# Attention shares: two tiles for the transposed blocks, later products, and reciprocals in pairs

## The chip, the cores and the metric

The kernel runs on one core of one Trainium2 chip. The metric is device time in microseconds (us) of one launch, as the median of several runs. The engines are named as in the profile: PE multiplies matrices (PEld is its weight load), DVE is the vector engine, ACT the scalar engine, POOL the GpSimd engine, and SP the engine on whose queue most DMAs are issued.

## What is computed

One encoder layer over 512 tokens and 16 learned meta tokens (528 keys) of width 2048, all in float32. Two groups of eight heads share one input projection: mixer A (grouped-query attention with normalised, rotated queries and keys) and mixer B (differential attention with a distance penalty). Each head's output is gated, all are projected once, normalised and added to the input.

```python
hn = rmsnorm(h, pre_norm_g)                       # h: 16 meta tokens + 512 tokens, 2048 wide
qa, ka, va, ga, qb, kb, vb, gb = split(hn @ w_in)
# mixer A, 8 heads of 128, 2 heads of keys and values
q, k = rope(rmsnorm(qa, q_g)), rope(rmsnorm(ka, k_g))
oa = softmax(q @ k.T / sqrt(128)) @ va
# mixer B, 8 heads, two score maps each
bias = -slope * abs(qpos - kpos)
a = softmax(q1 @ k1.T / 8 + bias) - lam * softmax(q2 @ k2.T / 8 + bias)
ob = rmsnorm(a @ vb, sub_g) * (1 - lambda_init)
y = concat(oa * silu(ga), ob * silu(gb)) @ w_out
out = h + rmsnorm(y, post_norm_g)                 # of the 512 tokens
```

## The kernel before

**Products.** Every float32 operand is split into a high part, which ACT rounds (`hi`, L337), and a rest, which DVE subtracts (`lo`, L340). A product is then three matmuls: high by high, rest by high, high by rest. Weights arrive in chunks of 512 KB: SP loads a chunk into the tile `st` (L149), ACT writes its high part `wh` (L156), DVE its rest `wl` (L157). Each of the three names has three buffers, and a chunk is asked for two chunks ahead of its use. The list `splits` holds the two instructions of every weight split in the order in which they are recorded.

**Stages.** A first block of projections up to about 40 us; then the eight heads of mixer B, each beside the projections of the next head (`dense_T`, written as `pd`); then the eight heads of mixer A beside their query projections and gates; from about 786 us the output projection (`po`).

**One head.** The 512 queries are taken in four tiles of 128 (`t`), two tiles to a half. For each tile PE writes scores into the only score buffer `sc`; DVE adds the penalty, stores them as `p` and takes the row maximum (L519 in mixer B, L618 in mixer A), which frees `sc`; ACT takes the exponential and its sum (L527, L621). In mixer B there are two score groups to a tile, and the shares of the two maps are joined by POOL (L532) and DVE (L534). DVE then transposes `p` in 32 by 32 blocks into the tile `pt` (L448, and L450 for the 16 meta keys). When both tiles of a half stand in `pt`, `regroup` writes `pt` to the DRAM tile `turn` (L455), reads it back in four pieces as `pl` (L461), and its meta block as `pmf` (L462): so the blocks land with the keys on the partitions. `pt` and `pmf` have one buffer each, `pl` has two.

**Shares by values.** `p_times_v` splits `pl` into `ph` (ACT, L337) and `pl` (DVE, L340), and the meta block into `pm`; then it multiplies them with the values: 13 matmuls `pv`, broken up by other work. In mixer B a head ends with `finish_B`: the squares of its output are summed by two matmuls `ss`, ACT takes the root (L559), DVE four reciprocals of 128 columns each (L562) and two products (L563, L564), and SP stores the gated head `gB` (L566).

**What sets the order.** PE's order is written out by the class `Lanes`: all matmuls stay in program order, and a clock that only counts matmul time decides when the next step of a head (a generator) is recorded between the matmuls of the projections. The waits of these steps are the numbers of `LAG`: `pB` and `pA` between the end of a half and the start of `p_times_v`, `pvB` and `pvA` between its splits and its matmuls, `scB` between score groups. SP's weight loads stay in program order too (`load`). On ACT, DVE, POOL and for the other DMAs the order is a scheduler's, which goes by priorities; weight splits have a raised one (`rank`). `tc.issue_after(x)` places the instructions of its block behind `x` on the engine of `x`. Each engine works through its own list in order, so that an instruction that waits holds up all behind it.

Of the kernel before, what the change touches and what calls it, by code (L numbers as in the profile page):

```python
# [10 lines left out]
F32 = mybir.dt.float32  # L11
F32R = mybir.dt.float32r
F16 = mybir.dt.float16
AF = mybir.ActivationFunctionType
ALU = mybir.AluOpType
AX = mybir.AxisListType

P = 128
# [10 lines left out]
DW = NT + (TT - 1) * P  # L29


LAG = dict(vals=3.5, bank=2.8, bankA=1.5, bankB=2.5, turnA=1.5, turnB=1.5, pvA=5.5, pvB=6.0, scB=3.0,
           pB=14.0, ss=6.0, qA=2.35, scA=5.1, pA=11.5, rope=10.2, head=3.85, fin=1.35, qn=1.4, norm=4.0, valsA=(10.0, 7.0),
           steps=(3.0, 2.5, 2.0, 2.0), stepsK=(2.5, 2.0, 1.5))

AHEAD = -60
# [70 lines left out]
def kernel(ctx: ExitStack, tc: tile.TileContext, xT, xn, xm, w_s, w_t, w_q, w_o,  # L107
                             gpre, gq, gk, lams, gsub, gpost, ident_d, cos_d, sin_d, dist_d, out):
    nc = tc.nc
# [12 lines left out]
    ap = att.enter_context(tc.tile_pool(name="ap", bufs=2))  # L122
# [38 lines left out]
    splits = []  # L161
# [101 lines left out]
    for t in (TT, 0, 1, 2, 3):  # L263
        rows = P if t < TT else NM
        src = xn[t * P:(t + 1) * P, :] if t < TT else xm
        for j in range(2 if t < 2 else 4):

            tag, w = ("pl", "ph")[j % 2], 1024
            if t >= 2:
                tag, w = ("f", "g", "ql")[t - 2], 512  # L270
            st = (gp if tag == "g" else ap).tile([P, w], F32, name="xns", tag=tag,
                                                 bufs=2 if t < 2 else 4)[:rows]
            load(st, src[:, j * w:(j + 1) * w])
            acc = ssx[:, t, j:j + 1] if t < TT else ssm[:, j:j + 1]
            if j % 2:
                nc.vector.tensor_tensor_reduce(out=st, in0=st, in1=st, scale=1.0, scalar=0.0,
                                               op0=ALU.mult, op1=ALU.add, accum_out=acc)
            else:
                nc.scalar.activation(st, st, AF.Square, accum_out=acc)
# [9 lines left out]
                            op0=ALU.mult)  # L289
# [46 lines left out]
    def hi(dst, src):  # L336
        nc.scalar.activation(dst, src, AF.Copy)  # L337
# [89 lines left out]
        return g  # L427


    pv_last = [None]  # L430
    pv_open = [False]

    def whole():
# [18 lines left out]
    def regroup(pt):  # L452

        turn = dr.tile([P, 1088], F32, name="turn", tag="turn", bufs=3)
        nc.sync.dma_start(out=turn, in_=pt)  # L455
        turn = turn.rearrange("(i k) r -> k i r", i=4)
        pl = ap.tile([P, 1024], F32R, name="pl", tag="pl")
        pm = ap.tile([32, 2 * P], F32, name="pmf", tag="pmf", bufs=1)
        quad = pl.bitcast(F32).rearrange("p (i r) -> p i r", i=4)
        for m in range(4):  # L460
            nc.sync.dma_start(out=quad[32 * m:32 * m + 32], in_=turn[:, :, 256 * m:256 * m + 256])  # L461
        nc.sync.dma_start(out=pm.rearrange("p (i r) -> p i r", i=4), in_=turn[:, :, 1024:])  # L462
        return pl, pm

    def p_times_v(regrouped, v, done, gate_of):

        vh, vl, vm = v
        ab = "B" if gate_of is None else "A"
        pl, pf = regrouped
        ph = ap.tile([P, 1024], F32R, name="ph", tag="ph")  # L470
        pm = ap.tile([96, 2 * P], F32R, name="pm", tag="pm", bufs=1)
        pt = pl.bitcast(F32)
        hi(ph, pt)
        lo(pl, pt, ph)
        hi(pm[0:32], pf)
        nc.gpsimd.tensor_scalar(out=pm[32:64], in0=pm[0:32].bitcast(F32), scalar1=1.0,  # L476
                                scalar2=1.0, op0=ALU.mult, op1=ALU.mult)
        lo(pm[64:96], pf, pm[0:32])
        yield LAG["pv" + ab]
        while gate_of is not None and not place(gate_of):  # L480
            yield 0.3
        pv_open[0] = True
        pv = ptr.tile([P, 512], F32, name="pv", tag="tr")
        o = pv[:, :2 * P]
        ph, pl = [t.rearrange("p (i c r) -> p c i r", i=4, c=TT) for t in (ph, pl)]
        for c in range(TT):
            mm(o, vh[:, c, :], ph[:, c], start=(c == 0), stop=False)
            mm(o, vl[:, c, :], ph[:, c], start=False, stop=False)
            mm(o, vh[:, c, :], pl[:, c], start=False, stop=False)
            if c % 2:  # L490
                yield 0.0
        mm(o, vm, pm, start=False, stop=True)
        pv_open[0] = False
        done(o)
# [7 lines left out]
    def attention_B(h, qs, ks, v, v_task):  # L502
        o = ap.tile([P, SEQ], F32, name="oB", tag="f", bufs=4)
        last = None
        for half in range(2):
            pt = ap.tile([P, 1088], F32, name="pt", tag="pt", bufs=1)
            for t in (2 * half, 2 * half + 1):
                tq = slice(t * P, (t + 1) * P)
                mx = ap.tile([P, 2], F32, name="mx", tag="mx", bufs=4)
                sm = ap.tile([P, 2], F32, name="sm", tag="sm", bufs=4)  # L510
                p2 = []
                for m, ((q, ql), s) in enumerate(zip(qs, ks)):
                    sc = psc.tile([P, 2, 512], F32, name="sc", tag="sc")
                    for i, (n0, n1) in enumerate(KEYS):
                        mm(sc[:, i, :HALF], q[:, tq], s[:, n0:n1], start=True, stop=False)
                        mm(sc[:, i, :HALF], ql[:, tq], s[:, n0:n1], start=False, stop=True)
                    p = ap.tile([P, NT], F32, name="p", tag="p", bufs=4)
                    w0 = 3 * P - 32 * t
                    nc.vector.tensor_tensor_reduce(  # L519
                        out=two(p), in0=sc[:, :, :HALF], in1=two(dist[:, w0:w0 + NT]),  # L520
                        scale=-0.125 / slope(h), scalar=3.0e38, op0=ALU.add, op1=ALU.min,
                        accum_out=mx[:, m:m + 1])
                    p2.append(p)
                    if m == 0:
                        yield LAG["scB"]
                for m in range(2):
                    nc.scalar.activation(p2[m], p2[m], AF.Exp, scale=-1.0,  # L527
                                         bias=mx[:, m:m + 1], accum_out=sm[:, m:m + 1])
                nc.vector.reciprocal(out=sm, in_=sm)  # L529
                c2 = ap.tile([P, 1], F32, name="c2", tag="c2", bufs=4)  # L530
                nc.vector.tensor_tensor(out=c2, in0=sm[:, 1:2], in1=nlam, op=ALU.mult)
                nc.gpsimd.tensor_scalar(out=p2[0], in0=p2[0], scalar1=sm[:, 0:1], scalar2=1.0,  # L532
                                        op0=ALU.mult, op1=ALU.mult)
                nc.vector.scalar_tensor_tensor(out=p2[0], in0=p2[1], scalar=c2, in1=p2[0],  # L534
                                               op0=ALU.mult, op1=ALU.add)
                turned(pt, p2[0], t % 2)
                if t % 2 == 0:
                    yield LAG["scB"]
            last = spawn_pv(v_task, p_times_v(regroup(pt), v, lambda pv, half=half:
                            nc.scalar.activation(half_of(o, half), by_quad(pv), AF.Copy), None),  # L540
                            LAG["pB"])
            if half == 0:
                yield LAG["scB"]
        over[h] = lanes.spawn(finish_B(h, o), LAG["fin"], last)

    def finish_B(h, o):
# [12 lines left out]
        nc.scalar.activation(sq, ss, AF.Sqrt, scale=1.0 / P, bias=epst)  # L559
        for t in range(TT):  # L560
            tq = slice(t * P, (t + 1) * P)
            nc.vector.reciprocal(out=sq[:, tq], in_=sq[:, tq])  # L562
        nc.vector.tensor_tensor(out=o, in0=o, in1=sq, op=ALU.mult)  # L563
        nc.vector.scalar_tensor_tensor(out=gB[h], in0=o, scalar=sgc, in1=gB[h],  # L564
                                       op0=ALU.mult, op1=ALU.mult)
# [25 lines left out]
    def attention_A(h, qn, q_task, k, k_task, v, v_task):  # L591
# [12 lines left out]
        kh, kl = k  # L604
        last = None
        for half in range(2):
            pt = ap.tile([P, 1088], F32, name="pt", tag="pt", bufs=1)
            for t in (2 * half, 2 * half + 1):
                tq = slice(t * P, (t + 1) * P)
                mx = ap.tile([P, 1], F32, name="mxA", tag="mx", bufs=4)  # L610
# [2 lines left out]
                for i, (n0, n1) in enumerate(KEYS):  # L613
# [1 line left out]
                    mm(sc[:, i, :HALF], qh[:, tq], kl[:, n0:n1], start=False, stop=False)  # L615
                    mm(sc[:, i, :HALF], ql[:, tq], kh[:, n0:n1], start=False, stop=True)
                p = ap.tile([P, NT], F32, name="p", tag="p", bufs=4)
                nc.vector.tensor_tensor_reduce(  # L618
                    out=two(p), in0=sc[:, :, :HALF], in1=two(zed[0][:, :NT]), scale=-ASCALE,
                    scalar=3.0e38, op0=ALU.add, op1=ALU.min, accum_out=mx)  # L620
                nc.scalar.activation(p, p, AF.Exp, scale=-1.0, bias=mx, accum_out=sm)  # L621
                nc.vector.reciprocal(out=sm, in_=sm)
                nc.gpsimd.tensor_scalar(out=p, in0=p, scalar1=sm, scalar2=1.0,
# [18 lines left out]
    def squares(raw, n, rows=P):  # L642
        ss = ap.tile([P, 4], F32, name="ssh", tag="ssh", bufs=4)
        for i in range(n):
            jk = ap.tile([P, P], F16, name="jk", tag="jk", bufs=1)
            nc.scalar.activation(jk[:rows], raw[:, i, :], AF.Square, accum_out=ss[:rows, i:i + 1])
        rstd(ss[:rows, :n], ss[:rows, :n], P, rows)
        return ss
# [596 lines left out]
```

## Time and profile before

| | us |
|---|---|
| median of 3 runs (lowest to highest) | 953.71 (953.40 to 954.62) |
| the profiled execution: time | 949.57 |
| the profiled execution: span, first to last instruction | 947.8 |
| PE busy, weight loads busy | 888.2, 782.6 |
| DVE, ACT, POOL busy | 631.9, 497.1, 130.2 |
| mean granted clock of PE | 0.978 |

The page of the profile gives these sums, a strip of the span in 40 slices, and the chain of waits that ended last. Three further views of the trace are used: the waits by engine (who waited for whom, how long in total, how often, the longest one), the timeline of one engine (each instruction with its start, its duration, and in brackets the idle time before it and what ended it), and windows (busy time of each engine in a stretch, with the granted clock of PE; 0.50 is half speed). A matmul's shown duration is modelled; its cost in a stream is the distance to the next start. PE's line of 94% does not mean that 94% of the span is needed.

### The profile page before, as it was taken

The page shows a single profiled execution, that of the slowest core. Times are in us where ns is not written, and L with a number is a line of the kernel's source. Part 1 is how long each engine was busy: PE and PEld are TensorE (multiplying, and loading weights), DVE is VectorE, ACT ScalarE, POOL GpSimd, SP SyncE. Part 2 cuts the span into 40 slices and gives each one's busy share as a digit, 9 for nine tenths or more (in the row PEclk, how much of TensorE's full clock was granted, in tenths as well). Part 3 has the DMA queues.
Part 4 walks back from the last instruction along what each step waited for, and adds up shares of the span by engine and source line. Part 5 has one row for each costly group of instructions (what it writes and reads, how often), then busy time and mean ns, then how long its engine had stood idle before and what let it go on. Part 6 is the DMA issues. An engine that isn't in the chain of part 4 may idle for free.

```text
span 947.8 us, 14079 instructions
## 1 busy us (share of the span) xinstructions
PE 888.2 (94%) x5130; PEld 782.6 (83%) x5130; DVE 631.9 (67%) x1137; ACT 497.1 (52%) x845; POOL 130.2 (14%) x168
## 2 busy tenths in 40 slices
PE   9999888989989899898998999998999799999996
PEld 8898787888978889788888888997888587888885
DVE  6586674756657557575576546678766575886786
ACT  6464553635527346363464353555757455764561
POOL 0102110021110211102101020224122110000010
PEclk9999999899999999999999999999999899999999
DMA  9838648596784867848634333454657557989884
GB/s 338 271 114 247 182 136 225 144 252 181 206 228 132 246 176 192 249 140 218 188 101 141 98 89 99 160 176 138 161 161 224 156 171 273 328 284 311 272 263 155
DMA packets 80677, 185.49 MB, mean 196 GB/s; under 512 B 15136, under 2 KB 38560, under 8 KB 80224
## 3 DMA queue, kind: packets, MB, share of 16 engines
q1 hardware_dynamic: 75856, 167.81, 54.2%
q0 software_dynamic: 4608, 16.78, 10.4%
q8 instruction: 40, 0.66, 0.3%
q14 instruction: 29, 0.24, 0.1%
q10 hardware_dynamic: 144, 0.01, 0.0%
HBM read 158.34 MB, written 59.77 MB: 230 GB/s over the span
## 4 chain that ended last, share of the span: by engine, by line
PE 60%; DMA 14%; DVE 12%; ACT 6%; issue 4%; POOL 2%; SPq 2%; DVEq 0%; ACTq 0%; POOLq 0%
PE pd L61 36%; PE po L61 15%; DMA turn<-pt 7%; PE pv L61 4%; DMA pl<-turn 4%; PE sc L61 4%; DVE sq L562 2%; DVE wl L157 2%; ACT ph L337 1%; DMA st<-in_w_t_dram 1%; DVE pt L448 1%; SPq L461 1%; DVE pl L340 1%; DMA ws<-in_w_o_dram 1%; DMA ws<-ws 1%
## 5 line engine op out<-in xcount | busy, mean ns | idle before, releaser
L61 PE MATMUL pd<-xh,wh 128*128 128x264 f32 (+1 forms) x992 | 330.5, 333 | 6.4 <-ACT wh L156 6.4
L61 PE MATMUL pd<-xl,wh 128*128 128x264 f32 (+1 forms) x992 | 327.4, 330 | 0.4 <-DVE xl L192 0.4
L61 PE MATMUL pd<-xh,wl 128*128 128x264 f32 (+1 forms) x992 | 326.1, 329 | 0.0
L157 DVE TENSOR_TENSOR wl<-st,wh 128x1024 fp32r<-128x1024 f32 (+2 forms) x159 | 191.4, 1205 | 101.4 <-ACT wh L156 100.4
L156 ACT ACTIVATE wh<-st 128x1024 fp32r<-128x1024 f32 (+2 forms) x159 | 165.0, 1040 | 178.4 <-PE pd L61 83.8
L61 PEld LDWEIGHTS pd<-xh,wh 128*128 128x128 f32 x992 | 190.4, 192 | 19.7 <-ACT wh L156 6.8
L61 PEld LDWEIGHTS pd<-xh,wl 128*128 128x128 f32 x992 | 189.7, 191 | 17.1 <-DVE wl L157 0.9
L61 PEld LDWEIGHTS pd<-xl,wh 128*128 128x128 f32 x992 | 190.4, 192 | 12.0 <-DVE xl L192 0.6
L527 ACT ACTIVATE p<-p,mx 128x528 f32<-128x528 f32 x64 | 47.1, 736 | 75.3 <-DVE mx L519 74.5
L448 DVE STREAM_TRANSPOSE pt<-p 128x512 f32<-128x512 f32 x64 | 45.3, 707 | 30.3 <-DMA turn<-pt 18.9
L61 PE MATMUL pv<-ph,vh 128*128 128x256 f32 x128 | 38.5, 301 | 16.0 <-ACT ph L337 13.3
L519 DVE CUSTOM_DVE_ANT_0 p<-sc,dist 128x528 f32<-128x528 f32 x64 | 44.7, 698 | 11.7 <-PE sc L61 11.6
L340 DVE TENSOR_TENSOR pl<-pl,ph 128x1024 fp32r<-128x1024 f32 x32 | 39.5, 1233 | 17.4 <-ACT ph L337 17.2
L61 PE MATMUL pd<-wh,xh 128*128 128x512 f32 x128 | 50.5, 394 | 0.0
L337 ACT ACTIVATE ph<-pl 128x1024 fp32r<-128x1024 f32 x32 | 33.6, 1049 | 32.0 <-DMA pl<-turn 32.0
L61 PE MATMUL pd<-wl,xh 128*128 128x512 f32 x128 | 49.9, 390 | 0.0
L61 PE MATMUL pd<-wh,xl 128*128 128x512 f32 x128 | 49.9, 390 | 0.0
L532 POOL TENSOR_SCALAR p<-p,sm 128x528 f32<-128x528 f32 x32 | 24.1, 752 | 183.7 <-DVE sm L529 183.7
L61 PE MATMUL pv<-pl,vh 128*128 128x256 f32 x128 | 39.3, 307 | 10.6 <-DVE pl L340 10.6
L476 POOL TENSOR_SCALAR pm<-pm 32x256 fp32r<-32x256 f32 x32 | 29.0, 906 | 134.9 <-ACT pm L337 98.7
L621 ACT ACTIVATE p<-p,mxA 128x528 f32<-128x528 f32 x32 | 23.6, 736 | 43.8 <-DVE mxA L618 43.6
L61 PE MATMUL sc<-s,q 128*128 128x264 f32 x128 | 35.7, 299 | 11.4 <-DVE mx L519 8.6
(223 smaller groups left out, 1562.8 us busy)
## 6 DMA issues: line engine op xcount, KB each, us to landing
st<-in_w_t_dram SPq DMA_DIRECT2D x82, 512.0 KB, 5.4
turn<-pt SPq DMA_DIRECT2D x32, 544.0 KB, 3.1
ws<-in_w_o_dram POOLq DMA_DIRECT2D x32, 512.0 KB, 8.5
pl<-turn SPq DMA_DIRECT2D x128, 128.0 KB, 4.0
st<-ws SPq DMA_DIRECT2D x32, 512.0 KB, 4.5
st<-in_w_o_dram SPq DMA_DIRECT2D x22, 512.0 KB, 4.6
ws<-in_w_o_dram SPq DMA_DIRECT2D x16, 512.0 KB, 5.3
ws<-ws SPq DMA_DIRECT2D x16, 512.0 KB, 5.1
```

Of the source, the lines that this page charges most:

```text
L61: self._add(self.nc.tensor.matmul(out, lhsT, rhs, start=start, stop=stop, **kw), us)
L156: splits.append((nc.scalar.activation(wh[:, c], st[:, c], AF.Copy), nc.vector.tensor_tensor(out=wl[:, c], in0=st[:, c], in1=wh[:, c].bitca ...
L157: nc.vector.tensor_tensor(out=wl[:, c], in0=st[:, c], in1=wh[:, c].bitcast(F32), op=ALU.subtract)))
L337: nc.scalar.activation(dst, src, AF.Copy)
L340: nc.vector.tensor_tensor(out=dst, in0=src, in1=h.bitcast(F32), op=ALU.subtract)
L448: nc.vector.transpose(pt[:, :1024].rearrange("p (m c t q) -> p c m t q", m=4, c=TT, t=2)[:, :, :, j], p[:, NM:].rearrange("p (c m q) -> p ...
L476: nc.gpsimd.tensor_scalar(out=pm[32:64], in0=pm[0:32].bitcast(F32), scalar1=1.0, scalar2=1.0, op0=ALU.mult, op1=ALU.mult)
L519: nc.vector.tensor_tensor_reduce(out=two(p), in0=sc[:, :, :HALF], in1=two(dist[:, w0:w0 + NT]), scale=-0.125 / slope(h), scalar=3.0e38, op ...
L527: nc.scalar.activation(p2[m], p2[m], AF.Exp, scale=-1.0, bias=mx[:, m:m + 1], accum_out=sm[:, m:m + 1])
L532: nc.gpsimd.tensor_scalar(out=p2[0], in0=p2[0], scalar1=sm[:, 0:1], scalar2=1.0, op0=ALU.mult, op1=ALU.mult)
L562: nc.vector.reciprocal(out=sq[:, tq], in_=sq[:, tq])
L621: nc.scalar.activation(p, p, AF.Exp, scale=-1.0, bias=mx, accum_out=sm)
```

## The change

Six edits:

- `pt` gets two buffers, and its first 32 partitions take the meta block back from DRAM (`pm = pt[:32, :2 * P]`); the tile `pmf` goes.
- `ph` has one buffer instead of two.
- The high parts `ph` and `pm` of the shares are held behind the last recorded weight split on ACT.
- The lags before the shares are used grow: `pB` from 14 to 22, `pA` from 11.5 to 16; `pvA` falls from 5.5 to 5.
- The four reciprocals of `finish_B` are held behind the last recorded row maximum on DVE, with a wait of `scB` after the second.
- The scratch tile `jk` of the squares is float32 instead of float16, and the first loads of `xn` use `pt` instead of `ph`.

```diff
-           pB=14.0, ss=6.0, qA=2.35, scA=5.1, pA=11.5, ...
+           pB=22.0, ss=6.0, qA=2.35, scA=5.1, pA=16.0, ...
-    pv_last = [None]
+    pv_last, maxima = [None], []
...
 def regroup(pt):
         turn = dr.tile([P, 1088], F32, name="turn", tag="turn", bufs=3)
         nc.sync.dma_start(out=turn, in_=pt)
...
-        pm = ap.tile([32, 2 * P], F32, name="pmf", tag="pmf", bufs=1)
+        pm = pt[:32, :2 * P]
...
         nc.sync.dma_start(out=pm.rearrange("p (i r) -> p i r", i=4), in_=turn[:, :, 1024:])
...
 def p_times_v(regrouped, v, done, gate_of):
         pl, pf = regrouped
-        ph = ap.tile([P, 1024], F32R, name="ph", tag="ph")
+        ph = ap.tile([P, 1024], F32R, name="ph", tag="ph", bufs=1)
...
-        hi(ph, pt)
+        with tc.issue_after(splits[-1][0].ins):
+            hi(ph, pt)
+            hi(pm[0:32], pf)
         lo(pl, pt, ph)
-        hi(pm[0:32], pf)
...
-            pt = ap.tile([P, 1088], F32, name="pt", tag="pt", bufs=1)
+            pt = ap.tile([P, 1088], F32, name="pt", tag="pt")
...
-                    nc.vector.tensor_tensor_reduce(
+                    maxima.append(nc.vector.tensor_tensor_reduce(
...
         for t in range(TT):
             tq = slice(t * P, (t + 1) * P)
-            nc.vector.reciprocal(out=sq[:, tq], in_=sq[:, tq])
+            with tc.issue_after(maxima[-1].ins):
+                nc.vector.reciprocal(out=sq[:, tq], in_=sq[:, tq])
+            if t == 1:
+                yield LAG["scB"]
```

What this does to the order is shown at three places. The first is ACT in the fifth head of mixer B (head 4), from the values' high part `vh` to the copy of the first product (`oB<-pv`); `s1`, `s2` are the next head's keys. Before:

```order
L337 ACTIVATE vh_3287<-tr_3363 128x512
L156 ACTIVATE wh_3390<-st_3388 128x1024
L337 ACTIVATE vm_3289<-tr_3400 16x128 x2
L337 ACTIVATE ph_3353<-pl_3152 128x1024
L337 ACTIVATE pm_3354<-pmf_3153 32x256
L540 ACTIVATE oB_3024<-pv_3429 128x4x64
```

ACT at the same place in the changed kernel:

```order
L337 ACTIVATE vh_3278<-tr_3346 128x512
L156 ACTIVATE wh_3373<-st_3371 128x1024
L337 ACTIVATE ph_3430<-pl_3139 128x1024
L337 ACTIVATE vm_3280<-tr_3383 16x128 x2
L337 ACTIVATE pm_3431<-pt_2996 32x256
L156 ACTIVATE wh_3449<-st_3447 128x1024
L337 ACTIVATE s1_3440<-kf_3437 64x528
L337 ACTIVATE s2_3441<-kf_3437 64x528
L156 ACTIVATE wh_3479<-st_3477 128x1024
L542 ACTIVATE oB_2995<-pv_3489 128x4x64
```

The split of the shares stands at the same chunk of weights as before, and between it and the product two weight splits and the keys' high parts have come. On PE, counted in the two orders, 178 matmuls of 264 columns and five transposes stand between the last score group of the first half and its first `pv` before; 190 such, 32 matmuls of 512 columns and the transposes stand there now.

The second place is DVE early in the sixth head of mixer B (head 5), where head 4 is finished: `sq` holds the roots whose reciprocals are taken, an ISA row that ends in `sc` is the row maximum of one score group, and `sm` the sums of the exponentials. Before:

```order
L519 ISA p_3637,mx_3605<-sc_3632,dist_558 128x528
L519 ISA mx_3605 128x1
L562 RECIPROCAL sq_3585<-sq_3585 128x128 x3
L529 RECIPROCAL sm_3606<-sm_3606 128x2
L562 RECIPROCAL sq_3585<-sq_3585 128x128
L531 TENSOR_TENSOR c2_3642<-sm_3606,nlam_557 128x1
L519 ISA p_3678,mx_3671<-sc_3673,dist_558 128x528
```

DVE there in the changed kernel:

```order
L521 ISA p_3697,mx_3650<-sc_3692,dist_558 128x528
L521 ISA mx_3650 128x1
L531 RECIPROCAL sm_3651<-sm_3651 128x2
L533 TENSOR_TENSOR c2_3702<-sm_3651,nlam_557 128x1
L536 SCALAR_TENSOR_TENSOR p_3657<-p_3697,c2_3702,p_3657 128x528
L521 ISA p_3757,mx_3750<-sc_3752,dist_558 128x528
L521 ISA mx_3750 128x1
L448 STREAM_TRANSPOSE pt_3573<-p_3657 128x4x4x32
L450 STREAM_TRANSPOSE pt_3573<-p_3657 128x32
L566 RECIPROCAL sq_3644<-sq_3644 128x128 x4
L521 ISA p_3799,mx_3750<-sc_3794,dist_558 128x528
```

The reciprocals stood between the maxima of the second and the third score group; now they stand between those of the fifth and the sixth, behind two transposes, and all four together.

The third place is ACT near the end of mixer A, around head 7's first exponentials: `p` rows are exponentials, `qh` is head 7's queries, `gt` a gate, `oA5` the copy of head 5's products. Head 5's second share split, `ph_7500`, stands two rows ahead of these; `ph_7606` is head 6's first. Before:

```order
L621 ACTIVATE p_7519,smA_7511<-p_7519,mxA_7510 128x528
L337 ACTIVATE qh_7538<-tr_7540 128x4x4x32
L621 ACTIVATE p_7572,smA_7564<-p_7572,mxA_7563 128x528
L629 ACTIVATE oA5_7475<-pv_7582 128x4x64
L580 ACT_TABLE_LOAD
L580 ACTIVATE gt_7772<-gt_7772 128x512
L337 ACTIVATE ph_7606<-pl_7399 128x1024
L337 ACTIVATE pm_7607<-pmf_7400 32x256
L621 ACT_TABLE_LOAD
L621 ACTIVATE p_7625,smA_7617<-p_7625,mxA_7616 128x528
L156 ACTIVATE wh_7445<-st_7443 128x1024
L156 ACTIVATE wh_7549<-st_7547 128x1024
```

ACT there in the changed kernel:

```order
L635 ACTIVATE oA5_7392<-pv_7393 128x4x64
L627 ACTIVATE p_7490,smA_7482<-p_7490,mxA_7481 128x528
L337 ACTIVATE qh_7508<-tr_7510 128x4x4x32
L627 ACTIVATE p_7542,smA_7534<-p_7542,mxA_7533 128x528
L156 ACTIVATE wh_7424<-st_7422 128x1024
L337 ACTIVATE ph_7465<-pl_7263 128x1024
L337 ACTIVATE pm_7466<-pt_7183 32x256
L156 ACTIVATE wh_7519<-st_7517 128x1024
```

Before, the share splits `ph_7500` and `ph_7606` both stand ahead of the weight split `wh_7445`. Now the weight split of the same place, `wh_7424`, stands ahead of head 5's second share split, `ph_7465`, but behind head 7's first exponential, `p_7542` (`p_7572` before). Line numbers of the changed kernel are two to six higher than those of the kernel before.

More of the change, by code (lines that the diff above doesn't have):

```diff
@@ L29 @@
 DW = NT + (TT - 1) * P
-LAG = dict(vals=3.5, bank=2.8, bankA=1.5, bankB=2.5, turnA=1.5, turnB=1.5, pvA=5.5, pvB=6.0, scB=3.0,
-           pB=14.0, ss=6.0, qA=2.35, scA=5.1, pA=11.5, rope=10.2, head=3.85, fin=1.35, qn=1.4, norm=4.0, valsA=(10.0, 7.0),
+LAG = dict(vals=3.5, bank=2.8, bankA=1.5, bankB=2.5, turnA=1.5, turnB=1.5, pvA=5.0, pvB=6.0, scB=3.0,
+           pB=22.0, ss=6.0, qA=2.35, scA=5.1, pA=16.0, rope=10.2, head=3.85, fin=1.35, qn=1.4, norm=4.0, valsA=(10.0, 7.0),
            steps=(3.0, 2.5, 2.0, 2.0), stepsK=(2.5, 2.0, 1.5))
@@ L266 @@
         for j in range(2 if t < 2 else 4):
-            tag, w = ("pl", "ph")[j % 2], 1024
+            tag, w = ("pl", "pt")[j % 2], 1024
             if t >= 2:
@@ L518, in attention_B @@
                     w0 = 3 * P - 32 * t
-                    nc.vector.tensor_tensor_reduce(
+                    maxima.append(nc.vector.tensor_tensor_reduce(
                         out=two(p), in0=sc[:, :, :HALF], in1=two(dist[:, w0:w0 + NT]),
                         scale=-0.125 / slope(h), scalar=3.0e38, op0=ALU.add, op1=ALU.min,
-                        accum_out=mx[:, m:m + 1])
+                        accum_out=mx[:, m:m + 1]))
                     p2.append(p)
@@ L606, in attention_A @@
         for half in range(2):
-            pt = ap.tile([P, 1088], F32, name="pt", tag="pt", bufs=1)
+            pt = ap.tile([P, 1088], F32, name="pt", tag="pt")
             for t in (2 * half, 2 * half + 1):
@@ L617, in attention_A @@
                 p = ap.tile([P, NT], F32, name="p", tag="p", bufs=4)
-                nc.vector.tensor_tensor_reduce(
+                maxima.append(nc.vector.tensor_tensor_reduce(
                     out=two(p), in0=sc[:, :, :HALF], in1=two(zed[0][:, :NT]), scale=-ASCALE,
-                    scalar=3.0e38, op0=ALU.add, op1=ALU.min, accum_out=mx)
+                    scalar=3.0e38, op0=ALU.add, op1=ALU.min, accum_out=mx))
                 nc.scalar.activation(p, p, AF.Exp, scale=-1.0, bias=mx, accum_out=sm)
@@ L644, in squares @@
         for i in range(n):
-            jk = ap.tile([P, P], F16, name="jk", tag="jk", bufs=1)
+            jk = ap.tile([P, P], F32, name="jk", tag="jk", bufs=1)
             nc.scalar.activation(jk[:rows], raw[:, i, :], AF.Square, accum_out=ss[:rows, i:i + 1])
```

## The prediction, made before the changed kernel was run

> **What bounds the kernel now.** I read the page's sums first, then the windows, then the waits by engine, then the timeline at the longest waits.
>
> ```profile
> span 947.8 us, 14079 instructions
> PE 888.2 (94%) x5130; PEld 782.6 (83%) x5130; DVE 631.9 (67%) x1137; ACT 497.1 (52%) x845; POOL 130.2 (14%) x168
> 269.90:330.20 60.30, 55.76 (x360) 50.98 (x359) 37.93 (x70) 30.15 (x47) 9.39 (x11) 0.98 0.74 206
> 800.00:850.00 50.00, 50.00 (x222) 41.42 (x221) 38.03 (x45) 34.08 (x47) 0.00 (x0) 1.00 0.90 314
> ```
>
> The windows' columns are the stretch, its length, the busy time of PE, PEld, DVE, ACT and POOL, PE's granted clock, the DMA share and GB/s. The first window is one head of mixer B: PE is busy 55.8 of 60.3 us and nothing else comes near, so PE's list sets the pace. DMA is no bound there: 206 GB/s, where the output stage moves 314. What can be won is what PE's list loses to waits and to half clock.
>
> ```profile
> ACT wh L156 <- PE pd L61: 83.8, 39, 4.4
> ...
> PE pv L61 <- ACT ph L337: 13.3, 6, 3.5
> ...
> PE pv L61 <- DVE pl L340: 10.6, 12, 2.5
> ...
> PE sc L61 <- DVE mx L519: 8.6, 11, 3.1
> ...
> PE pd L61 <- ACT wh L156: 6.4, 1, 6.4
> ...
> PE pv L61 <- DVE vm L340: 2.6, 1, 2.6
> ```
>
> These give total us, times and the longest wait. The products `pv` wait 13.3 + 10.6 + 2.6 = 26.5 us in 19 waits, the scores 8.6, and one weight split costs 6.4.
>
> ```profile
> 324.13 0.28 PE L61 MATMUL pd<-xl,wh 128*128 128x264 f32 x1
> 324.25 0.28 PE L61 MATMUL pd<-xh,wl 128*128 128x264 f32 x1
> 327.16 0.39 PE L61 MATMUL pv<-ph,vh 128*128 128x256 f32 x1 [2.63 <-DVE vm L340]
> 327.39 0.28 PE L61 MATMUL pv<-ph,vl 128*128 128x256 f32 x1
> 328.45 0.39 PE L61 MATMUL pv<-pl,vh 128*128 128x256 f32 x1 [0.78 <-DVE pl L340]
> ```
>
> A matmul of this width costs 0.12 us in a stream (324.13 to 324.25). The wait shown as 2.63 costs 327.16 - 324.25 - 0.12 = 2.79, and the next step is 0.23 instead of 0.12. So a wait loses some 0.27 more than its bracket.
>
> Behind such waits PE runs at half clock (column PEclk):
>
> ```profile
> 165.90:172.70 6.80, 5.65 (x14) 4.43 (x15) 3.81 (x8) 3.82 (x8) 0.85 (x1) 0.50 0.48 154
> ...
> 268.30:271.70 3.40, 3.40 (x17) 3.40 (x18) 0.32 (x1) 0.00 (x0) 0.41 (x2) 0.50 0.98 314
> 329.70:333.10 3.40, 3.40 (x18) 3.40 (x17) 0.00 (x0) 0.38 (x1) 1.27 (x2) 0.51 0.87 271
> ...
> 449.20:452.60 3.40, 3.40 (x16) 3.40 (x17) 0.47 (x1) 0.00 (x0) 0.20 (x1) 0.50 0.97 303
> ...
> 749.60:756.40 6.80, 3.55 (x8) 2.35 (x9) 5.44 (x9) 5.02 (x7) 1.77 (x2) 0.50 0.02 5
> sum 37.40, PE 32.09 PEld 28.99 DVE 16.40 ACT 12.18 POOL 7.55; mean PE 3.57 PEld 3.22 DVE 1.82 ACT 1.35 POOL 0.84
> ```
>
> The nine spells hold 32.1 us of PE work at half speed, so 16.0 is lost; one spell of 3.4 costs 1.7.
>
> **Later use of the shares.** Why `pv` waits at 327.16 the chain and the engines' timelines show:
>
> ```profile
> 321.92 1.75 SPq L461 DMA_DIRECT2D pl<-turn  x4
> 326.05 1.06 ACT L337 ACTIVATE ph<-pl 128x1024 fp32r<-128x1024 f32 x1 [3.87 <-DMA pl<-turn]
> 327.17 1.23 DVE L340 TENSOR_TENSOR pl<-pl,ph 128x1024 fp32r<-128x1024 f32 x1
> ```
>
> The pieces are asked for at 321.92 and `ph` starts only at 326.05, having held ACT for 3.87 us. The releaser `vm` in PE's bracket had long been done; `ph` ends at 327.11, and 327.16 follows. The rest, `pl`, comes 1.2 us later and makes the second wait. With the new lags some 30.9 us of matmuls stand between the last scores of a half and its `pv`, where 22.1 stood (190 of 264 columns and 32 of 512 for 178 of 264, transposes included). That is 8.8 us later, against a lateness of 2.8 + 0.9; the longest single wait is 3.5. So A = 26.5 + 19 x 0.27 = 31.6 us goes, where the split itself is in time. The hold puts `ph` behind a weight split of 1 us. In mixer B that one needs only PE work that ends 7.6 to 15 us ahead of the `pv`, and two splits and `pl` take 3.3 (1.00 + 1.06 + 1.23): covered. I take no cost there; without that cover it is the slower rival below.
>
> What stays in A: in the first three heads the waits come while weights load slowly (at 165.9 the half clock follows a weight chunk, not a share). I leave G = 5.0 of A there, six waits of the size of the one at 328.45 (6 x 0.78 = 4.7; bounds 0 and 10), and I count the 5.65 / 2 = 2.8 of the spell at 165.9 as staying. So E = 16.0 - 2.8 = 13.2 goes.
>
> **Two tiles `pt`, meta block read into the tile.** SP's queue waits for the tile `pmf`:
>
> ```profile
> SPq L462 <- DVE pm L340: 19.7, 12, 4.7
> ```
>
> These 19.7 us go, and DVE's transposes no longer wait for the store of the half before. Neither is a wait of PE, so the gain is 0 by itself; it lets the shares leave sooner, which A needs. Held longer, `pt` is free again when its meta block is split, ahead of the first transpose of the next head's same half. One buffer less of `ph` is 0: one split follows the other by half a head, some 30 us. The float32 scratch is an output that nothing reads: 0, bounds -1 and +1. At the queues, `pt`'s store now stands behind two weight requests on SP (the four at 321.92 took 0.44 each): up to 0.8 us more for the shares, inside the 8.8.
>
> **Reciprocals.**
>
> ```profile
> 294.23 0.39 PE L61 MATMUL ss<-sh,ones_r 128*128 128x512 f32 x1
> ...
> 296.94 2.58 DVE L562 RECIPROCAL sq<-sq 128x128 f32<-128x128 f32 x3 [1.86 <-ACT sq L559]
> 299.46 0.93 DVE L562 RECIPROCAL sq<-sq 128x128 f32<-128x128 f32 x1
> 300.35 0.69 DVE L519 CUSTOM_DVE_ANT_0 p<-sc,dist 128x528 f32<-128x528 f32 x1
> 301.11 0.39 PE L61 MATMUL sc<-s,q 128*128 128x264 f32 x1 [0.91 <-DVE mx L519]
> ```
>
> The row maximum at 300.35 stands behind four reciprocals (2.58 + 0.93), and the scores at 301.11 wait 0.91 for it. This recurs once a head (six times 0.91 is 5.5; 3.1 more in the first). The order shows that all four stay together, not in pairs, but later, ahead of another score group. From the last `ss` to the freed score buffer it takes 301.11 - 294.23 = 6.9 us; the next scores now stand 7.6 us of matmuls behind `ss`, where 5.8 stood. So B = 8.6 goes, with only 0.7 us to spare. Were ACT's root 1 us later, 0.3 a head would come back.
>
> **End of mixer A.**
>
> ```profile
> 746.12 0.28 PE L61 MATMUL sc<-kh,qlA 128*128 128x264 f32 x1
> 752.81 0.80 PE L61 MATMUL pd<-xh,wh 128*128 128x512 f32 x1 [6.41 <-ACT wh L156]
> ...
> 746.44 0.71 DVE L618 CUSTOM_DVE_ANT_0 p<-sc,zed 128x528 f32<-128x528 f32 x1
> ...
> 748.32 1.04 ACT L337 ACTIVATE ph<-pl 128x1024 fp32r<-128x1024 f32 x1
> ...
> 750.98 0.74 ACT L621 ACTIVATE p<-p,mxA 128x528 f32<-128x528 f32 x1
> 751.62 0.19 ACT L621 ACTIVATION_READ_ACCUMULATOR p<-p,mxA 128x1 f32 x1
> 751.71 1.99 ACT L156 ACTIVATE wh<-st 128x1024 fp32r<-128x1024 f32 x2
> ```
>
> Here the weight split stood last on ACT, behind a gate, a share split and an exponential. In the changed order it comes earlier, ahead of the shares: D = 752.81 - 746.12 - 0.12 = 6.6 goes. What is late next is head 5's second `ph`: it stands behind that weight split, which stands behind head 7's first exponential, which needs head 7's first scores; and its `pv` stands only 0.7 us of matmuls behind these scores. From the last score matmul: 0.32 to the maximum, 0.71 for it, 0.93 for the exponential, 1.0 for the weight split, 1.04 for `ph`: 4.0, less 0.7 is 3.3; `pl` behind it 0.9, and one spell of half clock 1.7. F = 5.9 comes back (bounds 0, if the scheduler's list is served while PE is late anyway, and 8).
>
> **Sum.** A 31.6 + B 8.6 + D 6.6 + E 13.2 = 60.0 goes; G 5.0 and F 5.9 come back: 49.1 net. No matmul is added or removed. The span becomes 947.8 - 49.1 = 898.7; the profiled run's time was 949.57, 1.8 over its span, so 900.5; the median of the runs was 4.1 over that one: **904.6**, said as 904. If every wait and half-clock spell named went, and nothing came back, it would be some 62.8 off: 891; with G's and F's lower bounds and small waits not listed, 886 is the floor.
>
> **Rivals.** *Shares still late.* Half of A and E stays (15.8 + 6.6), because the shares are held by DMA traffic or by the queue and not by when PE asks: 904.6 + 22.4 = 927. For it: `ph` waited 3.87 us for its pieces. Against: they were asked for 4 us before, and 8.8 us are added.
>
> *Slower: the hold.* Weight splits themselves wait for PE to free their tile (83.8 us in 39 waits, the longest 4.4). If that is freed too late, each of the 16 products of mixer B waits 1.00 + 1.06 + 1.23 = 3.3 us plus 1.7 at half clock, 80 in all, in place of A and E: 953.7 - 8.6 - 6.6 + 80 - 44.8 = 974. It decides from the point at which the tile is freed less than 3.3 us ahead of `pv`; the order shows 7.6 and more in mixer B.
>
> *Half speed stays.* It follows waits of 2.63 + 0.78 close together (spell at 329.70), so I let it go with them:
>
> ```profile
> 266.88 0.39 PE L61 MATMUL pv<-ph,vh 128*128 128x256 f32 x1 [3.46 <-ACT ph L337]
> 508.56 0.39 PE L61 MATMUL pv<-pl,vh 128*128 128x256 f32 x1 [2.52 <-DVE pl L340]
> 508.00:512.00 4.00, 3.44 (x28) 3.44 (x29) 0.96 (x3) 0.38 (x1) 0.00 (x0) 1.00 0.75 214
> ```
>
> A single wait of 2.52 left full clock. If only single waits of about 3.5 and more slow the clock, the spells at 268.30, 449.20 and 749.60 go, (3.40 + 3.40 + 3.55) / 2 = 5.2, the other 8.0 of E have another cause and stay: 912.6. [...]
>
> *It doesn't do what it says.* The reciprocals are not in pairs, and the 0.7 to spare doesn't hold: 0.9 in seven heads, 6.4, comes back: 911.
>
> **How the numbers follow.** Chances: forecast 0.52, half speed stays 0.05, reciprocals unchanged 0.10, shares still late 0.20, slower by the hold 0.08, and 0.05 for a gain of under 15 us, of which 0.03 is within 0.2% (about what a measurement of this kernel can tell from no change). Faster by over 0.2% sums to 0.52 + 0.05 + 0.10 + 0.20 + 0.02 = 0.89, slower 0.08. The range goes from the floor, 886, to 930, which takes in shares still late at its price.
>
> **What would show it.** Right: no wait of `pv` for `ph` or `pl` above 1 us from the third head on; no half clock in mixer B after 180 us; no wait of `sc` for `mx` once a head; near the end of mixer A a wait of `pv` of some 3 us in place of the wait for `wh`. Wrong: `pv` waiting for `ph` with ACT idle behind a weight split; DVE's reciprocals between a score group's end and its maximum; PE waits for `wh` or `wl` in mixer B.

## The result, and the profile after

The changed kernel took **908.48 us** (median of 4 runs, 905.28 to 914.89) beside 954.16 us for the kernel before on the same chip: a ratio of 0.9514, 95% interval 0.9443 to 0.9585. In a second, later measurement it took 910.59 beside 956.50: 0.9524 (0.9485 to 0.9563). So the change makes the kernel 4.8% faster, some 46 us. The profiled execution went from 949.57 to 910.12 us, its span from 947.8 to 908.3, which is 39.5 us: the one lies 4.6 us under its median and the other 1.6 over, so the profiles show some 6 us less than the medians.

The page's sums and the windows of two heads of mixer B after the change (stretch, length, busy time of PE, PEld, DVE, ACT, POOL, PE's granted clock, DMA share, GB/s):

```profile
span 908.3 us, 14068 instructions
...
PE 877.6 (97%) x5130; PEld 777.5 (86%) x5130; DVE 633.0 (70%) x1137; ACT 498.6 (55%) x844; POOL 126.7 (14%) x168
...
317.08:371.81 54.73, 54.70 (x363) 50.15 (x362) 39.24 (x71) 30.61 (x47) 8.03 (x11) 1.00 0.79 227
371.81:426.40 54.59, 54.30 (x360) 49.69 (x358) 38.03 (x70) 30.62 (x47) 9.04 (x11) 1.00 0.80 221
```

A head takes 54.7 us where it took 60, with the same matmuls and PE's clock at 1.00 throughout: within these heads PE has nothing left to win but matmuls. PE's waits, after:

```profile
PE sc L61 <- DVE mx L521: 6.6, 4, 5.9
PE sc L61 <- ACT qh L337: 5.2, 2, 3.1
PE pv L61 <- DMA st<-in_w_t_dram: 2.9, 1, 2.9
PE sc L61 <- ACT q L337: 2.2, 1, 2.2
PE sc L61 <- DVE l L340: 1.5, 2, 1.0
...
PE pv L61 <- DVE pl L340: 0.9, 1, 0.9
PE sc L61 <- DVE qlA L340: 0.8, 3, 0.3
```

The waits of `pv` fell from 26.5 us in 19 to 3.8 us in two, both at one place near the end of mixer A. The wait for `wh` (6.4) is gone. The waits of `sc` for `mx` are down from 8.6 to 6.6 only, but they are others: one of 5.9 us makes up nearly all of it. That one is new, and POOL's, DVE's and PE's timelines show its chain:

```profile
167.35 0.81 POOL L809 DMA_DIRECT2D ws<-in_w_o_dram  x1 [8.72 <-DMA ws<-ws]
168.25 0.70 POOL L534 TENSOR_SCALAR p<-p,sm 128x528 f32<-128x528 f32 x1
...
168.99 0.77 DVE L536 SCALAR_TENSOR_TENSOR p<-p,c 128x528 f32<-128x528 f32 x1 [6.85 <-POOL p L534]
...
171.53 0.66 DVE L521 CUSTOM_DVE_ANT_0 p<-sc,dist 128x528 f32<-128x528 f32 x1
...
172.26 0.59 PE L61 MATMUL sc<-s,q 128*128 128x264 f32 x1 [5.89 <-DVE mx L521]
```

POOL's list stands at the issue of a DMA (it adds to a sum of output weights and must wait for the DMA that writes that sum). The product for the shares stands behind it; DVE's list waits for that product; and the row maximum that frees the score buffer stands behind on DVE. POOL sits idle for 8.72 us, and from its product on DVE works off what stands ahead of the maximum, 3.3 us (168.99 to 172.26), before PE goes on. In the profiled execution of the second measurement the same wait is 5.57 us, so it belongs to this order and is not the chance of one execution.

The place where the prediction expected a new wait, in PE's and ACT's timelines:

```profile
705.34 0.39 PE L61 MATMUL pd<-xh,wl 128*128 128x512 f32 x1
708.65 0.39 PE L61 MATMUL pv<-ph,vh 128*128 128x256 f32 x1 [2.92 <-DMA st<-in_w_t_dram]
...
710.10 0.58 PE L61 MATMUL pv<-pl,vh 128*128 128x256 f32 x1 [0.94 <-DVE pl L340]
...
705.88 0.73 ACT L627 ACTIVATE p<-p,mxA 128x528 f32<-128x528 f32 x1 [2.62 <-DVE mxA L624]
...
706.61 1.04 ACT L156 ACTIVATE wh<-st 128x1024 fp32r<-128x1024 f32 x1
707.56 1.04 ACT L337 ACTIVATE ph<-pl 128x1024 fp32r<-128x1024 f32 x1
```

Exponential, weight split and `ph` follow each other on ACT without a gap, and `pv` starts 0.05 us after `ph` ends. The releaser in the bracket (a DMA) is the one inferred from semaphores; ACT's rows show that it is `ph`.

Five spells of half clock lie ahead of the kernel's tail, the first, the last and the sum of their windows being:

```profile
169.70:176.50 6.80, 4.24 (x19) 4.24 (x20) 6.80 (x13) 0.83 (x2) 0.00 (x0) 0.50 0.62 143
...
709.00:715.80 6.80, 5.86 (x21) 5.02 (x20) 5.18 (x8) 2.30 (x4) 1.25 (x1) 0.50 0.68 215
sum 23.80, PE 20.30 PEld 18.04 DVE 19.57 ACT 6.67 POOL 4.10; mean PE 4.06 PEld 3.61 DVE 3.91 ACT 1.33 POOL 0.82
```

Half of 20.3, 10.2 us, is lost there; it was 16.0.

### The profile page after: what moved, and what is told of

Its sections match the earlier page's. It is cut to its first block, busy times and chain, and to the rows that moved or that the text cites. A ratio compares the mean times of both kernels' runs of the same rounds, so it can differ in the third digit from the quotient of the medians.

```text
span 908.3 us, 14068 instructions
## 1 busy us (share of the span) xinstructions
PE 877.6 (97%) x5130; PEld 777.5 (86%) x5130; DVE 633.0 (70%) x1137; ACT 498.6 (55%) x844; POOL 126.7 (14%) x168
## 3 DMA queue, kind: packets, MB, share of 16 engines
q0 software_dynamic: 4608, 16.78, 10.7%
## 5 line engine op out<-in xcount | busy, mean ns | idle before, releaser
L448 DVE STREAM_TRANSPOSE pt<-p 128x512 f32<-128x512 f32 x64 | 45.2, 706 | 10.7 <-POOL p L629 9.9
L809 POOL DMA_DIRECT2D ws<-in_w_o_dram x32 | 26.6, 841 | 121.9 <-DMA ws<-ws 54.2
L629 POOL TENSOR_SCALAR p<-p,smA 128x528 f32<-128x528 f32 x32 | 25.8, 806 | 122.1 <-DVE smA L628 118.4
L536 DVE SCALAR_TENSOR_TENSOR p<-p,c 128x528 f32<-128x528 f32 x32 | 24.5, 766 | 21.4 <-POOL p L534 21.2
```

The costliest lines, as they stand in the source:

```text
L448: nc.vector.transpose(pt[:, :1024].rearrange("p (m c t q) -> p c m t q", m=4, c=TT, t=2)[:, :, :, j], p[:, NM:].rearrange("p (c m q) -> p ...
L809: nc.gpsimd.dma_start(out=dst, in_=src, accum_op=ALU.add)
```

## The experiments

The twelve runs take the change apart. Ratios are to the kernel before on the same chip, so they compare across chips.

| lags | hold of ph | tiles | new reciprocals | us | ratio (95%) |
|---|---|---|---|---|---|
| new | no | no | no | 916.77 | 0.9585 (0.9543 to 0.9628) |
| old | no | yes | no | 952.47 | 0.9962 (0.9935 to 0.9989) |
| new | yes | no | no | 904.61 | 0.9459 (0.9421 to 0.9496) |
| new | no | yes | no | 919.54 | 0.9613 (0.9577 to 0.9649) |
| new | yes | yes | no | 909.40 | 0.9518 (0.9488 to 0.9548) |
| new | no | yes | yes | 932.41 | 0.9750 (0.9719 to 0.9781) |
| old | yes | yes | yes | 935.19 | 0.9758 (0.9717 to 0.9798) |
| new | yes | yes | yes (the changed kernel, second measurement) | 910.59 | 0.9524 (0.9485 to 0.9563) |

**The lags alone.**

```diff
-           pB=14.0, ... pA=11.5      pvA=5.5
+           pB=22.0, ... pA=16.0      pvA=5.0
```

> The kernel before with the three new lags alone (pB 22, pA 16, pvA 5); tiles, hold and reciprocals as before. Theory 1 (the later use is what pays, and nothing else is needed): pv waits for ph and pl fall from 26.5 us to under 5, time 905 to 920. Theory 2 (the later use needs the second tile): the single tile pmf is now held up to 8.8 us longer, the wait of SP for pm grows from 19.7 us to over 60, weight loads behind it come late and PE waits for wh or wl in mixer B; time 930 or more.

916.8: theory 1. No wait of `pv` is left, SP's wait for the single meta tile grew only from 19.7 to 29.9 us, and PE waits for no weight in mixer B. So the second tile isn't what makes the later use possible. Three numbers in a table bring 40 us by themselves, where the whole change brings 46. The largest waits of PE that remain:

```profile
PE sc L61 <- DVE mx L519: 9.9, 12, 2.1
PE pd L61 <- ACT wh L156: 4.3, 1, 4.3
PE sc L61 <- ACT q L337: 4.2, 5, 2.1
```

**The tiles alone.** The changed kernel with the old lags, `hi(ph, pt)` without the hold, and the old reciprocals.

> The changed kernel with the old lags, without the hold of ph and with the reciprocals of before: the two tiles pt, the meta block in them and the single ph remain. Theory 1: no gain by itself, pv still waits about 26 us, time 945 to 955. Theory 2 (the store of the half before and the tile pmf were what made the shares late): pv waits fall below 13 us, time 930 or less.

952.5, a gain of 0.1 to 0.7%: theory 1. `pv` still waits 16.6 us for `ph` and 9.0 for `pl`. The float32 scratch and the moved loads of `xn` are in this run too, so they and the tiles are worth no more than this together.

**The old reciprocals in the changed kernel.**

```diff
-            with tc.issue_after(maxima[-1].ins):
-                nc.vector.reciprocal(out=sq[:, tq], in_=sq[:, tq])
-            if t == 1:
-                yield LAG["scB"]
+            nc.vector.reciprocal(out=sq[:, tq], in_=sq[:, tq])
```

> The changed kernel with the reciprocals of before (no hold, no wait between them). By the prediction's term B the scores wait 0.9 us a head for a maximum behind four reciprocals again: six or seven waits of sc for mx, 5 to 7 us more than the changed kernel, 913 to 916. Rival (this part does nothing, since the four stay together): within 2 us of the changed kernel. Second rival (the hold made the new wait of 5.9 us near 166 us): that wait goes and the time is 5 us lower.

909.4, the same as the changed kernel (0.9518 against 0.9514 and 0.9524): the first rival. Its PE waits hold the reason:

```profile
PE sc L61 <- DVE l L340: 6.4, 6, 1.5
...
PE sc L61 <- DVE mx L521: 1.4, 3, 1.0
```

With the old reciprocals the wait of 0.9 us a head behind them is gone as well, and so is the wait of 5.9 us; the scores wait for the queries' rest `l` six times instead, 1.1 us on average. PE's waits come to 22.5 us in all, where the two traces of the changed kernel have 21.5 and 22.8. It isn't a plain exchange, though: in the second of these two `l` takes 4.3 us as well, beside the wait of 5.57.

**No hold.**

```diff
-        with tc.issue_after(splits[-1][0].ins):
-            hi(ph, pt)
-            hi(pm[0:32], pf)
+        hi(ph, pt)
         lo(pl, pt, ph)
+        hi(pm[0:32], pf)
```

> The changed kernel with ph and pm not held behind a weight split (only the order of recording). In ACT's list ph then stands one weight split earlier. Theory 1 (lags suffice): pv waits stay under 4 us and the time within 3 us of 908. Theory 2 (the hold is needed): ph waits on ACT for its pieces ahead of a weight split, PE waits for wh in mixer B, time 915 or more. If the late pv at the end of mixer A comes from the hold, its 2.9 + 0.9 us go here, and with its half clock the time falls by 5 or 6.

932.4, some 22 us more than with it (0.9750 against 0.9514 and 0.9524): theory 2 in size, but the waits are not those it named. PE doesn't wait for `wh` in mixer B; it waits for the queries, 10.7 us for `q` and 5.8 for `l`, since ACT's weight split ahead of `q` waits for its chunk (such waits of ACT come to 18.3 us in four). The order on SP's queue had changed too: in three heads the second of two weight requests now stands ahead of `pt`'s store, where the changed kernel has it behind the store. The late `pv` at the end of mixer A went, as expected, but a wait for `wh` and `wl` of 2.5 + 1.8 us took its place.

```profile
PE sc L61 <- ACT q L337: 10.7, 4, 4.1
PE sc L61 <- DVE mx L520: 7.6, 4, 5.1
PE sc L61 <- DVE l L340: 5.8, 6, 1.4
```

The 5.1 us in the second row is the wait behind POOL's issue again, now at 176 us. So it doesn't come from the hold, and the second rival of the run before falls. Nor is it shown to come from the new reciprocals alone: with the old ones it is absent in the changed kernel, but the run with lags and hold and without tiles, below, has the same chain at 170 us, for 2.15 us.

**The hold with the old lags.**

> The changed kernel with the old lags (pB 14, pA 11.5, pvA 5.5); tiles, hold and reciprocals stay. If the later use is what pays (the kernel before with the lags alone took 917), pv waits for ph and pl of 25 us or more come back: 945 to 955. If the hold costs where the use is early (the slower rival: 1.00 + 1.06 + 1.23 + 1.7 a product), it is above the kernel before: 960 to 1000. If the hold pays by itself, 930 or less.

935.2, between the first case and the third, and nearer to the third. `pv` waits as much as ever (17.7 + 9.1 us), and yet 22 us are gone: the waits for `wh` at the end of mixer A (6.4), those for `q` and `l` in the first heads and those in the output projection, with some 3 us of half clock. ACT still stands at the shares' pieces for most of the time that it stood there with the tiles alone (30.3 us):

```profile
ACT ph L337 <- DMA pl<-turn: 24.4, 6, 5.7
```

So with the old lags the hold doesn't make the shares' data come in time. A likely reason for the gain is that a weight split now stands ahead of the share instead of behind it; that is argued from the order, not shown. The new reciprocals are in this run too, and no run has the hold with the old lags and the old reciprocals; the scores still wait 1.3 us a head for a maximum here. The second case, the slower rival, doesn't occur: `pv` waits 17.7 us for `ph` against 16.6 with the tiles alone, the longest 4.4 against 3.4. Lags alone (40 us) and this version (22) add up to more than the change brings: the two overlap.

**Lags and hold, without tiles.**

> The kernel before with the new lags and the hold of ph and pm behind the last weight split; one tile pt, the tile pmf, two ph and the old reciprocals. The lags alone took 916.8, the changed kernel 908.5. If the hold is what the lags lack, 908 to 911 (then tiles and reciprocals are worth nothing measurable). If the tiles are, 917 or more. By the order the late pv at the end of mixer A (3 + 1 us) comes with the hold.

904.6: the first case. It isn't slower than the changed kernel; its ratio of 0.9459 against 0.9514 and 0.9524 would be some 5 to 6 us less, but the intervals overlap. The late `pv` at the end of mixer A came with the hold, as expected (2.94 + 0.65 us). What the hold does shows in one row of ACT's waits. The lags alone, then lags and hold:

```profile
ACT ph L337 <- DMA pl<-turn: 19.9, 7, 5.3
```

```profile
ACT ph L337 <- DMA pl<-turn: 2.1, 2, 1.8
```

In the kernel before this row was

```profile
ACT ph L337 <- DMA pl<-turn: 32.0, 8, 4.7
```

With the later lags alone, the scheduler still put `ph` where its data might come, one weight split early, and ACT's whole list stood there for 19.9 us until the pieces had landed. Held behind the split, `ph` finds its data ready, and what stands behind it on ACT is no longer late: PE's waits for `q` (4.2 us with the lags alone), for `wh` at the end of mixer A (4.3) and for weights in the output projection (2.1) are gone, and the waits for `mx` fall from 9.9 to 5.8.

**Lags and tiles, without hold.**

> The new lags and the two tiles (with the single ph), without the hold and with the old reciprocals. The lags alone took 916.8; with tiles and new reciprocals and no hold it was 932.4. If the tiles without a hold make weight chunks land late (wh waits for st, then q), 925 to 935; if it was the reciprocals without a hold, 915 to 919; if tiles and hold are each worth half of the last 8 us, 912 to 914.

919.5, just over the second case: the tiles without the hold cost nothing measurable (0.9613 against 0.9585), and the new reciprocals without the hold cost 13 us (0.9750). With the hold they cost nothing (0.9524 against 0.9518). By the rows, the 13 us are 6 us more of PE's waits (37.1 against 30.9) and 7 more of half clock (18.2 against 10.8), the wait of 5.1 us behind POOL's issue and 5 more for `q` among them. Why the one order suits the reciprocals and the other doesn't, apart from weight chunks that ACT waits for 18.3 us instead of 6.5, wasn't separated.

**A later pv in mixer A.**

```diff
-           pvA=5.0, ... pA=16.0
+           pvA=6.0, ... pA=17.0
```

> The changed kernel with pA 17 and pvA 6 instead of 16 and 5. In the order head 5's second ph then no longer stands behind head 7's first exponential, and no other share or weight split falls short. Theory (the late pv at 705 us and the half clock behind it cost 3.1 + 1.1 + 2.9 = 7.1 us): that wait goes, the time falls to 900 to 903. Rival (the weight split or the chunk's DMA is late there anyway): a wait for wh of 3 us or more takes its place, 906 to 910.

902.8, ratio 0.9429 (0.9397 to 0.9461): the theory. No wait of `pv` is left. The interval lies apart from that of the changed kernel's second measurement (0.9485 to 0.9563), though not from that of its first (0.9443 to 0.9585). It is the lowest time measured, but its interval overlaps that of lags and hold without tiles. The wait near 166 us is still there (5.7 us).

**Sums of output weights later.** Some two fifths of POOL's summing DMAs are recorded in mixer A.

```diff
-            weigh(2)
+            weigh(1)
...
-                weigh(2)
+                weigh(1)
...
     for h in range(NH):
+        weigh([3, 2, 2, 2, 2, 2, 1, 0][h])
```

> The changed kernel with pA 17 and pvA 6 (902.8 before), and with some two fifths of the summing of output weights (DMAs that add, issued by POOL) moved from mixer B to mixer A. Theory: POOL's list waits less at these issues in mixer B and weight chunks land sooner, so the wait of 5.9 us near 166 us and its half clock (together 8) and the waits of q behind a late chunk go: 892 to 897. Rival (they have other causes, or come again in mixer A): 900 to 906.

915.3, slower than either side expected, though each is right about its stage. In mixer B the wait of 5.9 us is gone, there is no half clock at all, and from 100 to 400 us PE is busy 295.8 us, where the version with the same lags and the sums in their old place has 290.8. In mixer A the traffic rises (241 GB/s from 600 to 700 us instead of 169), and ACT waits for a late weight chunk:

```profile
697.69 0.58 ACT L337 ACTIVATE qh<-tr 128x512 fp32r<-128x512 f32 x1
708.29 1.06 ACT L156 ACTIVATE wh<-st 128x1024 fp32r<-128x1024 f32 x1 [10.03 <-DMA st<-in_w_t_dram]
709.26 1.04 ACT L337 ACTIVATE ph<-pl 128x1024 fp32r<-128x1024 f32 x1
...
710.35 0.58 PE L61 MATMUL pv<-ph,vh 128*128 128x256 f32 x1 [8.93 <-ACT ph L337]
```

Here the prediction's slower rival is seen at last: `ph` is tied to a weight split that is late, and PE waits 8.93 us for a share that needs nothing of that weight. It was the chunk's DMA that came late, not PE's release of the tile.

**The changed kernel again, and two without tiles.**

> The changed kernel once more, beside the three below on one chip. Every theory expects 905 to 912. If the wait near 166 us (a row maximum on DVE behind a product that POOL does late, since POOL's list stands at a DMA issue) is set by the order, it is here again at 2 us or more; if it was chance of one execution, it is not.

910.6; the wait is there again (5.57 us), so it belongs to the order.

> The kernel before with the lags pB 22, pA 16, pvA 6 and the hold; one tile pt, pmf, two ph and the old reciprocals. With pvA 5 it took 904.6. If the late pv at the end of mixer A costs 3.1 + 1.0 + half clock as in the changed kernel, 897 to 900; if the tiles and the reciprocals pay once this wait is gone, it is slower than the changed kernel with the later pvA (902.8).

908.6, not faster than with `pvA` 5 (0.9503 against 0.9459; the intervals overlap). The late `pv` went as expected, but PE waits 4.0 us for `wh` and 1.6 for `wl` in the output projection, where the version with `pvA` 5 has no such wait. A step of 1 us in a lag gains in one order and not in another. By its time it is slower than the changed kernel with the later `pv` (0.9429, intervals apart), which was the second case; but `pA` is 16 here and 17 there, and the waits that make it slower are these, so it doesn't show that the tiles or the reciprocals pay.

> The kernel before with the new lags and the hold (904.6 so far), and ph with one buffer instead of two. The tiles with the single ph cost some 5 us (909.4 against 904.6). If the single ph is the reason (ACT's next ph waits for the pv before, 5.7 us in two waits), 907 to 911; if it is the tiles or the meta block in them, 903 to 906.

910.0, and it doesn't answer its question. The first loads of `xn` share the tiles of `ph`; with a single one PE waited 3.5 us at 46 us, and a spell of half clock follows (1.7 us lost): 5.2 of the 6.5 us between the two profiled spans. In the heads PE's waits are those of the version with two, within 2 us. What the tiles cost beside the hold, if anything (0.9518 against 0.9459, and the intervals overlap), stays open.

## Why the prediction was right, point by point

The forecast was 904, the time 908.5. In the profiled executions 49.1 us were to go, and 39.5 went. That the medians come so close is in part luck: the profile after lies over its median and the one before under it, and by the rows the terms missed to both sides. The waits for `mx` came out 6.6 us worse than forecast, the half clock 5.7, and the scores' waits for the queries 4.0 (9.7 us in all, where the kernel before has 5.7, and the sum had no term for them); the waits of `pv` came out 5.4 us better, and 1.7 us of waits in the output projection went that the sum left standing. By what was left of each term:

| term | predicted to be left, us | left, us |
|---|---|---|
| waits of pv | 5.0 (first heads) + 4.2 (end of mixer A) | 0 + 3.8 |
| waits of sc for mx | 0 | 6.6 |
| wait of pd for wh | 0 | 0 |
| half clock | 2.8 + 1.7 | 10.2 |

- **Later use of the shares (A): right.** Lags alone took 40 us; A and E less G in the prediction come to 39.8, close, though not term by term (the scores still waited 9.9 us for maxima there). The 5.0 us that were to stay in the first heads didn't stay.
- **The wait for wh and what comes instead (D, F): right in place, mechanism and nearly in size.** 3.3 + 0.9 was said; 2.92 + 0.94 is in the brackets. Half clock behind it cost 5.86 / 2 = 2.9 instead of 1.7, since the spell lasted 6.8 us and not 3.4. Taking the wait away gave some 8 us (0.9524 or 0.9514 to 0.9429, on different chips). D is a gain of the hold, which the prediction doesn't say: with the new lags and no hold PE waits for `wh` and `wl` there in all three runs (4.3 + 0.6 us, and twice 2.5 + 1.8).
- **The hold, D apart, at no cost and no gain: wrong, the step that failed most.** "I take no cost there" priced it from the side of a loss alone. It is worth 9 us (0.9613 to 0.9518 with tiles) to 12 us (0.9585 to 0.9459 without), and 22 with the new reciprocals (0.9750 to 0.9524). The row was quoted: `ph` held ACT for 3.87 us. What the prediction priced was only PE's wait for `ph`, not what stood behind `ph` on ACT.
- **Reciprocals (B): half right.** The wait of 0.9 us a head went. It goes with the old reciprocals too where lags, tiles and hold are in (three waits for `mx`, 1.4 us); without the hold it takes the new ones (three waits of 0.9 us in mixer B with the old, none with the new); and with the old lags the new ones leave 1.3 us a head. So the place of the reciprocals alone doesn't decide. And the sum took a wait off without asking what else stands in DVE's list: the maximum near 171 us now stands behind a product of POOL, which stands behind a DMA. This new wait, with its half clock (4.24 / 2), costs 8 us at its place, about what B was to bring.
- **Half clock (E): too large a gain.** 4.5 us was to be left, 10.2 is. Each of the waits not foreseen (5.9 us for `mx`, 5.2 in two for `qh`, 3.2 for `q` and `l` in one head) has its spell.
- **Tiles: right**, nothing of weight by themselves. That they were needed for the later use was not so.
- **The signs.** Three of the four that were to show it right are there. The fourth, no half clock in mixer B after 180 us, is not: a spell begins at 272.10 us, and one at 327.5 in the second trace of the changed kernel.

Of the rivals, *shares still late* doesn't occur. *The hold* doesn't either, where it was looked for, and showed itself in another kernel. *Half speed stays* falls: in mixer B after 276 us there is neither a wait of over 0.5 us nor a spell in the first trace, and the one spell there in the second stands behind waits of 1.60 + 1.04 us for `q` and `l`. *The reciprocals aren't in pairs* is true of all eight heads: in each, all four stand between two neighbouring row maxima. The price that the rival put on it, 0.9 us a head, was not paid.

## What to carry to other kernels

An instruction that waited for a DMA was paid for here by what stood behind it on its engine's list: ACT stood at the shares' pieces for 32.0 us before, for 2.1 with lags and hold, and POOL's 8.72 us at one issue came out as a wait of 5.89 us on PE. So look for the engine that idles at a transfer, even where the matmuls wait for another name, and move the instruction behind work that is ready. A wait removed by reordering is only gone when the next list over has been read too; here a DMA issue of POOL, far off the bound, made a wait that with its half clock took 8 us. And traffic moved from a crowded stage to one that looks empty must be compared with that stage's own late transfers: with the sums moved there (241 GB/s from 600 to 700 us instead of 169), one late chunk held ACT for 10.03 us.

## What the runs showed of the hardware

In the changed kernel's clock record the five spells of half clock ahead of the tail begin at 169.70, 272.10, 613.44, 681.70 and 709.01 us; the three short ones last 3.413 us each, the first and the last 6.827. Counted in steps of 3.413 us, they begin 30, 130, 150 and 158 steps behind the first; those of the kernel before are 11, 23, 41, 59, 76, 94, 153 and 182 such steps behind its first, at 128.35. Two of these steps in each kernel, first of the changed one, then of the one before (the windows' columns as above):

```profile
678.27:681.68 3.41, 1.08 (x7) 0.80 (x7) 3.06 (x7) 2.12 (x4) 1.43 (x2) 1.00 0.02 5
681.68:685.10 3.42, 3.42 (x14) 3.03 (x13) 1.12 (x5) 0.83 (x2) 0.71 (x1) 0.50 0.72 256
```

```profile
507.22:510.63 3.41, 2.07 (x17) 2.08 (x18) 1.70 (x3) 0.00 (x0) 0.01 (x1) 1.00 1.03 322
510.63:514.05 3.42, 3.42 (x23) 3.08 (x23) 2.09 (x7) 1.45 (x2) 0.00 (x0) 1.00 0.08 17
```

In the first pair one wait of 2.12 us (for `qh`, up to 680.46) lies within the first step, and the second ran at 0.50. In the second pair PE had waited 2.52 us, up to 508.56, but 1.3 of it fell into this step and 1.2 into the one ahead, and the clock stayed at 1.00. The spell behind the late `pv` lasts two steps; PE's wait of 0.94 us for `pl`, up to 710.10, lies in the first (PE's busy time in the row is modelled):

```profile
709.01:712.42 3.41, 2.47 (x10) 2.03 (x9) 3.35 (x5) 0.84 (x1) 1.25 (x1) 0.50 0.54 159
712.42:715.83 3.41, 3.41 (x13) 3.02 (x12) 1.85 (x5) 1.48 (x3) 0.00 (x0) 0.50 0.83 275
```

These are single places. They show that the longer wait isn't always the one with half clock behind it: 2.12 us had it, at a price of 3.42 / 2 = 1.7 us more, and 2.52 had not. So the single wait of 2.52 us that left full clock, on which the prediction built a rival, does not show that waits of its length leave full clock elsewhere.
